# A bidirectional hybrid encoder layer: the scan's turns move from TensorE to VectorE and DMA, and the planner's step estimate is set anew

## The chip, the cores and the metric

The kernel runs on one core of one Trainium2 chip. The metric is the device time of one execution in microseconds (us), the median of several runs; less is better. TensorE (PE in the profile) does the matmuls, VectorE (DVE) and ScalarE (ACT) the elementwise work and the evacuation of PSUM, GpSimd (POOL) small work, and SyncE (SP) issues nearly all DMAs, in order, from one queue.

## What is computed

One encoder layer is applied to two request groups, 1024 and 256 tokens, with shared weights, in float32. The tokens go through one projection into three head groups: a scan in two directions (SSD, 16 heads of 64), windowed attention (8 heads of 64) and attention to a memory of 256 rows (4 heads of 128). The three results go side by side through the output projection. Cut to what bears on the change:

```python
def layer(x, mem, ...):
    proj = rms_norm(x, norm_g) @ w_in
    xbc, z_ssd, dt_raw, q, k, v, z_att, mq, z_mem = split_cols(proj, IN_SIZES)
    xbc = jax.nn.silu(centred_dwconv(xbc, conv_w, conv_b))
    xs, Bm, Cm = split_cols(xbc, ...)
    y_f = ssd_scan(xs, dt[:, :, 0], A[0], Bm, Cm)
    y_b = ssd_scan(xs[:, ::-1], dt[:, ::-1, 1], A[1], Bm[:, ::-1], Cm[:, ::-1])[:, ::-1]
    y = (y_f + y_b + d_skip[:, None] * xs).reshape(b, T, SSD_WIDTH)
    yg = (y * jax.nn.silu(z_ssd)).reshape(b, T, SSD_GROUPS, SSD_WIDTH // SSD_GROUPS)
    o_ssd = rms_norm(yg, ...)
    ...
    return x + jnp.concatenate([o_ssd, o_att, o_mem], axis=-1) @ w_out
```

## The kernel before

The 1280 tokens are ten tiles of 128 (t = 0 to 7 of the long group, 8 and 9 of the short one), in two groups of five. Every large product is done in three passes: both operands are split into a high and a low part (`wsplit`, line 338, for weights: ACT makes `wh`, DVE makes `wl`), and high x high, high x low and low x high are summed. So a weight tile `wraw` (SP's DMA, four buffers) turns into `wh` and `wl` (three buffers each) and then serves 15 matmuls, three for each of five token tiles. That is `block_tok` (line 368): 16 steps k over the 2048 input features, 512 output columns. Other products use seven multiplications for eight (`block_pair`, line 1327). The last of the projection's blocks and the output's blocks run in this order: kv, mq, z0, z1 for the first group; z0, z1, mq for the second; then four output blocks, the last two of them clear of other work; then `block_pair` for the second group of the output.

Beside the dense matmuls stand four *lanes*, queues of Python generators: `ATT` (attention, memory attention), `SSD` (`ssd_one`, `ssd_two`), `PREP` (preparations of q, k and memory) and `DEC` (`decay`). Every generator cuts its work into steps and yields `wants(tiles, banks, after)` ahead of a step: the tiles it will read, how many of the three shared PSUM banks (`mix`) it takes, and what must have been said to be done. After each piece of a dense block, `run` calls `pump` (line 301), which takes steps from the lanes in the order ATT, PREP, SSD, DEC, as far as `may` allows. All of this happens when the program is written: what decides is not the chip but `Clocks` (line 43), an estimate with one clock for each engine. `cost` (line 61) gives an instruction's time, `ran` (line 75) books it, `ready` (line 111) says whether the step's inputs are there by the clock of PE. The chip then runs the fixed order; a step put too early makes TensorE wait, one put too late makes its lane longer.

Some dates force a lane, whatever `ready` says. `refill_o` (line 1581), which loads the second operand of the output blocks during the second mq block, needs `ssd_two(5)` by k = 11; and at k = 9 of the third output block all lanes are emptied, since their memory is given back.

The scan. The convolution leaves its results in DRAM with features on rows, `xbc_d[12, 128, 1280]`. `ssd_one(t)` (line 948) loads two tiles `xc` of 128 features x 4 x 128 tokens each, one for each half of the heads, turns each by four 128x128 transposes on TensorE into a PSUM bank `pxs` (lines 974 to 977), and DVE copies it to `xs`, with tokens on rows. `ssd_two(t)` (line 1156) ends with the normed output `y`, tokens on rows. `turn_ssd` (line 1145) turns it back with four transposes into the bank `pr`, ACT copies it to `so`, and one DMA stores it to `oT_d[2 + g]`, features on rows, of shape [128, 4, 640] for each group of five tiles. `refill_o` and `seven_load` read these as rows of 640 values.

Of the kernel before, what the change touches and what calls it, by code (L numbers as in the profile page):

```python
# [19 lines left out]
P = 128  # L20
# [10 lines left out]

RATES = {'kv': (4, 4), 'mq0': (8, 8), 'z0': (8, 8), 'z1': (8, 8), 'mq1': (8, 8), 'o': (8, 8)}
DEBT = 6.0
AHEAD, QUEUE = 300.0, 4000.0
NEG = -1e30

UNITS = (0, 4, 1, 5, 2, 6, 7, 3, 8, 9)
# [5 lines left out]
class Clocks:  # L43
# [17 lines left out]
    def cost(self, e, ins, ops, power):  # L61
        n = max([self.size(x) for x in ops] or [1])
        if e == "PE":
            m = self.size(ops[0])
            one_pass = ops[-1].dtype == F32R or ops[1].dtype == F32R
            return m / 2.4 + 14 if one_pass else max(m / 0.6, 213) + 6
        if e == "DVE":
            return 150 + 1.05 * n
        if e == "ACT":
            return (190 + 0.8 * n if n > 16 else 190) + (190 if len(ins.outs) > 1 else 0)  # L70
        if e == "POOL":
            return 60 + 4.2 * n if n > 16 else 250 + 180 * n if power else 300
        return 50

    def ran(self, e, ins, power=False):
        outs, srcs = [[x.bass_ap for x in xs if hasattr(x, "bass_ap")] for xs in (ins.outs, ins.ins)]
        cost = self.cost(e, ins, outs + srcs, power)
        if e != "SP":
            self.now[e] = max(self.now[e], self.now["PE"])
        if not self.lane:  # L80
            self.now[e] += cost
            return
        at = self.now[e] if e != "SP" else self.now["PE"]
        for x in srcs:
            at = max(at, self.full.get(self.name(x), 0.0))
        for x in outs:
            at = max(at, self.free.get(self.name(x), 0.0))
        if e == "SP":
            end = at + 2600 + self.size(outs[0]) * 1.5
        else:  # L90
            end = self.now[e] = at + cost + 20
        for x in srcs:
            k = self.name(x)
            self.free[k] = max(self.free.get(k, 0.0), end)
        for x in outs:
            k = self.name(x)
            if e != "SP":
                self.free[k] = max(self.free.get(k, 0.0), end)
            self.full[k] = end + 90
# [10 lines left out]

    def ready(self, want):
        tiles, n = want[:2]
        at = [self.full.get(self.name(x), 0.0) - (0 if n else AHEAD) for x in tiles]
        at += [self.opens("mix", 3, i + 1) - 400 * i for i in range(n)]
        at += [self.now[e] - QUEUE for e in ("ACT", "DVE")]
        return max(at) <= self.now["PE"]

# [28 lines left out]
def wants(*tiles, banks=0, after=()):  # L146
    return tiles, banks, after
# [3 lines left out]
def hymba_encoder_kernel(  # L151
# [67 lines left out]
    def dram(shape, name):  # L219
        return dr.tile(shape, F32, tag=name, name=name)  # L220
# [4 lines left out]
    q_d = [dram([P, 512], f"q_{t}") for t in range(NT)]  # L225
    mq_d = [dram([P, 512], f"mq_{t}") for t in range(NT)]
    kv_d = [dram([P, 288], f"kv_{t}") for t in range(NT)]
    oT_d = [[dram([P, 4, 640], f"oT{c}_{g}") for g in range(2)] for c in range(4)]
    yp_d = [dram([P, 1024], f"yp_{t}") for t in range(NT)]
    sb_d = [dram([P, 1024], f"sb_{t}") for t in range(NT)]  # L230
    row_d = [[dram([P, 640], f"row{n}{k}") for n in "HL"] for k in range(KT)]
# [65 lines left out]
    def may(i):  # L297
        w = wanted[i]
        return owed[i] >= 1 and lanes[i] and (w is None or (said.issuperset(w[2]) and clk.ready(w)))

    def pump(rates):

        for i in range(4):
            owed[i] = min(owed[i] + rates[i % 2], DEBT) if lanes[i] else 0.0
        while True:
            i = next((j for j in (ATT, PREP, SSD, DEC) if may(j)), None)
            if i is None:
                return
            owed[i] -= 1
            step(i)  # L310
# [627 lines left out]
    def wb(name, dtype=F32, shape=(P, 512)):  # L938
        return mp.tile(list(shape), dtype, tag="wb", name=name, bufs=WBB)
# [4 lines left out]
    def prior(t, *part):  # L944
        i = SCAN.index(t)
        return (("decay", SCAN[i - 1]) + part,) if i else ()

    def ssd_one(t):
# [4 lines left out]
        S.dma_start(bc, xbc_d[8:12, :, tok].rearrange("f p c -> p f c"))  # L953
        xc = []
        for g in range(2):
            x = wb("xc", shape=(P, 4, P))
            S.dma_start(x, xbc_d[4 * g:4 * g + 4, :, tok].rearrange("f p c -> p f c"))
            xc.append(x)
        yield wants(bc, banks=1, after=prior(t, "weighed"))
        ps = psum("pcb")  # L960
# [10 lines left out]
        said.add(("ssd_one", t, "cb"))  # L971
        xsT = []
        for g in range(2):
            yield wants(xc[g], banks=1, after=prior(t) + (("dt_prep", t // 5 * 5),))
            ps = psum("pxs")
            for j in range(4):
                turned(ps[:, j * P:(j + 1) * P], xc[g][:, j, :])
            xt = mp.tile([P, 512], F32, tag="xs", name="xs", bufs=2)
            V.tensor_copy(xt, ps)
            xsT.append(xt)  # L980
        xs_of[t] = xsT
        yield wants(cb)
# [162 lines left out]
    def turn_ssd(g):  # L1145

        if g in last_y:
            t, y = last_y.pop(g)
            ps = psum("pr")
            for j in range(4):  # L1150
                T.transpose(ps[:, j * P:(j + 1) * P], y[:, j * P:(j + 1) * P], ident)
            o = mp.tile([P, 512], F32, tag="rb", name="so", bufs=RBB)
            A.activation(o, ps, AF.Copy)
            S.dma_start(oT_d[2 + g][t // 5][:, :, t % 5 * P:(t % 5 + 1) * P], hv(o, 4))

    def ssd_two(t):
        first = t in (NS - 1, NT - 1)
        last = t in (0, NS)
        tok = slice(t * P, (t + 1) * P)
        yield wants(after=(("decay", t // NS * NS),))  # L1160
        ss = sm.tile([P, 2], F32, tag="s2", name="yss", bufs=4)
        if not last:
            cc = mp.tile([P, 2, P], F32, tag="btok", name="cc", bufs=1)
            S.dma_start(cc, xbc_d[10:12, :, tok].rearrange("f p c -> p f c"))
        ld = []
        for g in range(2):
            c = slice(g * 512, (g + 1) * 512)

            y = mp.tile([P, 512], F32, tag="ya" if t % 2 else "rf", name="yd", bufs=2)
            S.dma_start(y, yp_d[t][:, c])  # L1170
            z = mp.tile([P, 512], F32, tag="xs", name="zd", bufs=2)
            S.dma_start(z, z_d[g][t])
            st = None
            if not first:
                st = state[:, c] if last else wb("st2")
                S.dma_start(st, sb_d[t][:, c])
            ld.append((y, z, st))
        yield wants(*([last_y["y"][2]] if "y" in last_y else []))
        norm_ssd()
        for g in range(2):  # L1180
            c = slice(g * 512, (g + 1) * 512)
            y, z, st = ld[g]
            yield wants(y, z, *(() if last else (cc, state)), banks=0 if last else 1)
            if not last:
                pf = psum("pyb")
                T.matmul(pf, cc[:, g, :], state[:, c], start=True, stop=True)
                y2 = wb("y3")
                V.tensor_mul(hv(y2), hv(pf), hb(eacs_all[:, t, 8 * g:8 * g + 8], 8, 64))
                V.tensor_add(y, y, y2)
            V.tensor_mul(y, y, z)  # L1190
            if not first and not last:
                V.tensor_mul(hv(state[:, c]), hv(state[:, c]), hb(cd_all[:, t, 8 * g:8 * g + 8], 8, 64))
                V.tensor_add(state[:, c], state[:, c], st)
            yield wants(y)
            A.activation(z, y, AF.Square, scale=0.5, accum_out=ss[:, g:g + 1])
            if g in last_y:
                yield wants(last_y[g][1], banks=1)
                turn_ssd(g)
        yield wants(ss)
        rs = sm.tile([P, 2], F32, tag="s2", name="yrs", bufs=4)  # L1200
        rsqrt(rs, ss, 1.0 / 512, 2)
        G.tensor_scalar(out=rs, in0=rs, scalar1=0.5, scalar2=None, op0=ALU.mult)
        last_y["y"] = t, [x[0] for x in ld], rs
        if first:
            yield wants(rs)
            norm_ssd()
            for g in range(2):
                yield wants(last_y[g][1], banks=1)
                turn_ssd(g)

    seven = {1: (0, 0, 0), 2: (0, 1, 5), 6: (1, 1, 2), 5: (1, 0, 1), 3: (1, 2, 6), 7: (0, 3, 3), 4: (0, 2, 4)}
# [2 lines left out]
    def seven_load(k):  # L1214

        q, j = divmod(k, 4)
        raw[k] = [rp.tile([P, 640], F32, tag="ch", name=n, bufs=CH) for n in ("ra", "rb_")]
        S.dma_start(raw[k][0], oT_d[q][1][:, j, :])
        S.dma_start(raw[k][1], oT_d[2 + q][1][:, j, :])

    def seven_sums(k):
        a, b = raw[k]
# [332 lines left out]
    def part(fn, *a, **kw):  # L1555
        return lambda: fn(*a, **kw)
# [24 lines left out]
    def refill_o(grp):  # L1581
        def f(q):
            need((attn, mem_attn, ssd_two, ssd_two)[q], [4 if q < 2 else 5])
            return [part(fill_direct, q, j, oT_d[q][grp][:, j, :],
                         gain=None if q < 2 else vec[:, R_SG + 4 * (q - 2) + j:R_SG + 4 * (q - 2) + j + 1])
                    for j in range(4)]
        return f
# [285 lines left out]
```

## Time and profile before

| | us |
|---|---|
| median of 3 runs | 1777.49 (1776.81 to 1780.14) |
| the profiled execution's own time | 1773.83 |
| its span, first to last instruction | 1772.1 |
| GpSimd busy | 683.8 |
| DMA, mean of the span | 177 GB/s |

The span is what lies between the first and the last instruction; 1.7 us more lie around it. A busy TensorE is not a TensorE at its peak: its matmuls are pipelined, their durations overlap, and only the distance from one start to the next tells what one costs. DVE and ACT overlap in the same way, though less. In a group's row, "x80" is the number of instructions, and three times stand for shortest, median and longest. The kernel records every instruction through one helper, line 128, so groups are told apart by their tiles. Three lines of the page that the prediction does not show:

```profile
DVE  5596788989968888797777877678776533766665
ACT  6554555445545444346787666658886532433332
DMA  8794454446544333376467766767785734644442
```

Each digit is a tenth of the busy share in one of 40 slices of 44 us; the lanes run from slice 18 to slice 33.

### The profile page before, as it was taken

What the parts mean: (1) busy time and instruction counts of PE and PEld (TensorE: products, weight loads), DVE (VectorE), ACT (ScalarE), POOL (GpSimd) and SP (SyncE); (2) the same over time, 40 slices, a digit from 0 to 9 for tenths busy, and PEclk for the clock granted to TensorE, in tenths of its full rate; (3) what the DMA queues carried; (4) which work ended last, traced back from release to release, by engine and by line L of the source; (5) the groups of instructions that cost most, each with busy time, mean ns of one, the idle gap of its engine ahead of it and who ended that gap; (6) DMA issues with size and microseconds to landing.
All of it is one profiled execution on the core that took longest, in us unless ns stands there. A gap on an engine that the chain in (4) does not pass through costs nothing.

```text
span 1772.1 us, 30974 instructions
## 1 busy us (share of the span) xinstructions
PE 1755.3 (99%) x10306; PEld 1572.0 (89%) x10306; DVE 1310.9 (74%) x2417; ACT 971.8 (55%) x2181; POOL 683.8 (39%) x1092
## 2 busy tenths in 40 slices
PE   9999999999999999999999999999999999999999
PEld 7889999999899999988788877887788888889999
DVE  5596788989968888797777877678776533766665
ACT  6554555445545444346787666658886532433332
POOL 0026798860478989220110000111200100068775
PEclk9999999999999999999999999999999999999999
DMA  8794454446544333376467766767785734644442
GB/s 293 238 319 175 136 149 148 128 143 194 156 119 145 119 104 106 90 216 208 143 188 249 259 213 192 226 190 230 243 249 161 222 110 147 207 142 147 145 144 77
DMA packets 210993, 313.23 MB, mean 177 GB/s; under 512 B 21584, under 2 KB 84368, under 8 KB 210832
## 3 DMA queue, kind: packets, MB, share of 16 engines
q1 hardware_dynamic: 210688, 311.19, 56.7%
q8 instruction: 81, 1.33, 0.3%
q14 instruction: 80, 0.66, 0.1%
q10 hardware_dynamic: 144, 0.06, 0.0%
HBM read 242.42 MB, written 68.75 MB: 176 GB/s over the span
## 4 chain that ended last, share of the span: by engine, by line
PE 88%; DMA 4%; DVE 3%; ACT 2%; issue 1%; POOL 1%; SPq 0%; ACTq 0%; DVEq 0%; POOLq 0%
PE acc L128 66%; PE accm L128 11%; PE py L128 2%; PE po L128 1%; PE psc L128 1%; PE pst L128 1%; PE pmo L128 1%; PE pms L128 1%; PE ppt L128 1%; DMA wraw<-in_w_in_laid_dram 1%; PE pyf L128 1%; DMA xst<-in_x_prompt_dram 1%; DVE wl L128 1%; PE pyb L128 0%; ACT lg L128 0%
## 5 line engine op out<-in xcount | busy, mean ns | idle before, releaser
L128 PE MATMUL acc<-wh,xH 128*128 128x512 f32 (+1 forms) x1248 | 490.0, 393 | 0.1
L128 DVE TENSOR_TENSOR wl<-wraw,wh 128x512 fp32r<-128x512 f32 (+1 forms) x480 | 355.5, 744 | 172.9 <-ACT wh L128 170.1
L128 PE MATMUL acc<-wl,xH 128*128 128x512 f32 (+1 forms) x1248 | 473.7, 380 | 0.7 <-DVE wl L128 0.5
L128 PE MATMUL acc<-wh,xL 128*128 128x512 f32 (+1 forms) x1248 | 472.1, 378 | 0.0
L128 ACT ACTIVATE wh<-wraw 128x512 fp32r<-128x512 f32 (+1 forms) x480 | 291.5, 613 | 211.6 <-PE acc L128 136.5
L128 POOL TENSOR_TENSOR ws<-wraw 128x128 f32<-128x128 f32 x224 | 156.9, 700 | 365.8 <-DMA wraw<-in_w_in_pairs_dram 163.1
L128 PEld LDWEIGHTS acc<-wl,xH 128*128 128x128 f32 x1248 | 234.7, 188 | 45.1 <-issue 6.5
L128 PEld LDWEIGHTS acc<-wh,xH 128*128 128x128 f32 x1248 | 234.6, 188 | 44.9 <-issue 7.0
L128 PEld LDWEIGHTS acc<-wh,xL 128*128 128x128 f32 x1248 | 234.2, 188 | 44.6 <-issue 1.0
L128 ACT ACTIVATE sh<-ws 128x384 fp32r<-128x384 f32 x224 | 115.5, 522 | 253.3 <-POOL ws L128 126.6
L128 DVE TENSOR_TENSOR sl<-ws,sh 128x384 fp32r<-128x384 f32 x224 | 158.7, 712 | 115.4 <-ACT sh L128 113.9
L128 POOL TENSOR_TENSOR ws<-wraw,ws 128x128 f32<-128x128 f32 x224 | 153.1, 683 | 17.2
L128 POOL TENSOR_TENSOR ws<-ws,wraw 128x128 f32<-128x128 f32 x224 | 154.3, 689 | 0.0
L128 POOL TENSOR_TENSOR wraw<-wraw 128x128 f32<-128x128 f32 x224 | 139.8, 624 | 17.1
L128 PE MATMUL acc<-xH,wl 128*128 128x320 f32 x320 | 100.0, 312 | 1.0 <-DVE wl L128 1.0
L128 PE MATMUL acc<-tH,sl 128*128 128x320 f32 x320 | 98.9, 309 | 0.0
L128 PE MATMUL acc<-xL,wh 128*128 128x320 f32 x320 | 98.9, 309 | 0.0
L128 PE MATMUL accm<-tH,wl 128*128 128x320 f32 x320 | 98.8, 309 | 0.0
L128 PE MATMUL acc<-tH,sh 128*128 128x320 f32 x320 | 98.7, 309 | 0.0
L128 PE MATMUL acc<-xH,wh 128*128 128x320 f32 x320 | 98.7, 309 | 0.0
L128 PE MATMUL accm<-tL,wh 128*128 128x320 f32 x320 | 98.5, 308 | 0.0
L128 PE MATMUL accm<-tH,wh 128*128 128x320 f32 x320 | 98.5, 308 | 0.0
(458 smaller groups left out, 3829.1 us busy)
## 6 DMA issues: line engine op xcount, KB each, us to landing
wraw<-in_w_in_pairs_dram SPq DMA_DIRECT2D x160, 256.0 KB, 2.7
wraw<-in_w_in_laid_dram SPq DMA_DIRECT2D x128, 256.0 KB, 3.6
wraw<-in_w_out_laid_dram SPq DMA_DIRECT2D x64, 256.0 KB, 3.1
wraw<-in_w_out_pairs_dram SPq DMA_DIRECT2D x64, 256.0 KB, 2.9
rf<-ac SPq DMA_DIRECT2D x40, 256.0 KB, 3.8
rb<-ac SPq DMA_DIRECT2D x40, 256.0 KB, 4.2
wraw<-in_w_mem_laid_dram SPq DMA_DIRECT2D x32, 256.0 KB, 4.7
ra<-in_x_turned_dram SPq DMA_DIRECT2D x16, 320.0 KB, 3.8
```

Source lines behind the costliest of these rows:

```text
L128: r = f(*a, **kw)
```

## The change

The diff has three parts. The scan's input tile is loaded by four DMAs, one for each 32 tokens, into the 32 rows that those tokens will have, in runs of 32 values (32x32 blocks, features on rows within a block); one DVE transpose of all 32x32 blocks then gives `xs`. The normed output is turned by one DVE transpose, and four DMAs put the blocks in their place in DRAM; the layout of `oT_d[2]` and `oT_d[3]` becomes [4, 128, 640]. Both steps take no PSUM bank any more.

The estimate gets other costs: for one-pass matmuls at least 85 ns, for others a share by the rows written; for DVE 67 + 1.04 n, for ACT 50 or 92 + 0.835 n and 92 for each further operand or output. An instruction's end no longer holds its engine for 20 ns, but its result counts as late by 110 ns (ACT) or 90 ns (DVE). A step that takes a bank is ready 700 ns after its inputs and 300 ns after the bank; one that takes none, at the time of its inputs (before: 300 ns ahead of it).

The order of the lanes becomes SSD, DEC, ATT, PREP between the end of `mem_attn(4)` and that of `ssd_two(5)`.

```diff
-AHEAD, QUEUE = 300.0, 4000.0
+MARGIN, QUEUE = {"PE": 700.0, "bank": 300.0, "other": 0.0}, 4000.0
+LATE = {"ACT": 110.0, "DVE": 90.0}
...
-            return m / 2.4 + 14 if one_pass else max(m / 0.6, 213) + 6
+            return max(m / 2.4 + 14, 85) if one_pass else max(m / 0.6, 213) * list(ops[0].ap)[0][1] / 128 + 6
         if e == "DVE":
-            return 150 + 1.05 * n
+            return 67 + 1.04 * n
         if e == "ACT":
-            return (190 + 0.8 * n if n > 16 else 190) + (190 if len(ins.outs) > 1 else 0)
+            aps = sum(hasattr(x, "bass_ap") for x in ins.ins)
+            return (50 if ops[-aps].space == "PSUM" else 92) + 0.835 * n + 92 * (aps - 1) + (92 if len(ins.outs) > 1 else 0)
...
-            end = self.now[e] = at + cost + 20
+            self.now[e] = at + cost
+            end = at + cost + LATE.get(e, 20)
...
-        at = [self.full.get(self.name(x), 0.0) - (0 if n else AHEAD) for x in tiles]
-        at += [self.opens("mix", 3, i + 1) - 400 * i for i in range(n)]
+        at = [self.full.get(self.name(x), 0.0) + MARGIN["PE" if n else "other"] for x in tiles]
+        at += [self.opens("mix", 3, i + 1) - 400 * i + MARGIN["bank"] for i in range(n)]
...
-    oT_d = [[dram([P, 4, 640], f"oT{c}_{g}") for g in range(2)] for c in range(4)]
+    oT_d = [[dram([P, 4, 640] if c < 2 else [4, P, 640], f"oT{c}_{g}") for g in range(2)] for c in range(4)]
...
-            i = next((j for j in (ATT, PREP, SSD, DEC) if may(j)), None)
+            late = ("mem_attn", 4) in said and ("ssd_two", 5) not in said
+            i = next((j for j in ((SSD, DEC, ATT, PREP) if late else (ATT, PREP, SSD, DEC)) if may(j)), None)
...
-            x = wb("xc", shape=(P, 4, P))
-            S.dma_start(x, xbc_d[4 * g:4 * g + 4, :, tok].rearrange("f p c -> p f c"))
+            x = wb("xc")
+            for a in range(4):
+                c = slice(t * P + 32 * a, t * P + 32 * a + 32)
+                S.dma_start(x[32 * a:32 * a + 32].rearrange("p (b j) -> p b j", j=32),
+                            xbc_d[4 * g:4 * g + 4, :, c].rearrange("f (q i) c -> i (f q) c", i=32))
...
-            yield wants(xc[g], banks=1, after=prior(t) + (("dt_prep", t // 5 * 5),))
-            ps = psum("pxs")
-            for j in range(4):
-                turned(ps[:, j * P:(j + 1) * P], xc[g][:, j, :])
+            yield wants(xc[g], after=prior(t) + (("dt_prep", t // 5 * 5),))
             xt = mp.tile([P, 512], F32, tag="xs", name="xs", bufs=2)
-            V.tensor_copy(xt, ps)
+            V.transpose(xt, xc[g])
...
-            ps = psum("pr")
-            for j in range(4):
-                T.transpose(ps[:, j * P:(j + 1) * P], y[:, j * P:(j + 1) * P], ident)
             o = mp.tile([P, 512], F32, tag="rb", name="so", bufs=RBB)
-            A.activation(o, ps, AF.Copy)
-            S.dma_start(oT_d[2 + g][t // 5][:, :, t % 5 * P:(t % 5 + 1) * P], hv(o, 4))
+            V.transpose(o, y)
+            for a in range(4):
+                c = slice(t % 5 * P + 32 * a, t % 5 * P + 32 * a + 32)
+                S.dma_start(oT_d[2 + g][t // 5][:, :, c].rearrange("f (q i) c -> i (f q) c", i=32),
+                            o[32 * a:32 * a + 32].rearrange("p (b j) -> p b j", j=32))
...
-                yield wants(last_y[g][1], banks=1)
+                yield wants(last_y[g][1])
...
-        S.dma_start(raw[k][1], oT_d[2 + q][1][:, j, :])
+        S.dma_start(raw[k][1], oT_d[2 + q][1][j])
...
-            return [part(fill_direct, q, j, oT_d[q][grp][:, j, :],
+            return [part(fill_direct, q, j, oT_d[q][grp][:, j, :] if q < 2 else oT_d[q][grp][j],
```

2 lines of the change are left out of this document (1 added, 1 removed).

## The prediction, made before the changed kernel had been run

> **What bounds the kernel now.** I read the page first: the shares of busy time and the chain that ended last.
>
> ```profile
> span 1772.1 us, 30974 instructions
> PE   1755.3 (99%) x10306; PEld 1572.0 (89%) x10306; DVE 1310.9 (74%) x2417; ACT 971.8 (55%) x2181; POOL 683.8 (39%) x1092
> q1 hardware_dynamic: 210688, 311.19, 56.7%
> PE 88%; DMA 4%; DVE 3%; ACT 2%; issue 1%; POOL 1%; SPq 0%; ACTq 0%; DVEq 0%; POOLq 0%
> ```
>
> TensorE leaves only 17 us of the span uncovered, and 88% of the chain is its own work. Work that leaves TensorE shortens the kernel; work added to another engine costs only where TensorE comes to wait for it. The page is an average, so I cut out the stretch in which the lanes (attention, scan, preparations) run between the dense matmuls, with the answer by windows; its columns are length, then busy time of PE, PEld, DVE, ACT, POOL, then clock, DMA share and GB/s.
>
> ```profile
> 766.00:1410.00 644.00, 634.90 (x3473) 516.54 (x3474) 486.95 (x1103) 447.81 (x1203) 76.85 (x148) 1.00 0.68 211
> 1410.00:1446.00 36.00, 36.00 (x199) 30.87 (x198) 13.64 (x29) 17.37 (x41) 0.00 (x0) 1.00 0.47 142
> ```
>
> The granted clock is 1.00, so nothing is to be won there. DVE is at 487/644 = 76% and DMA at 68%: both have room. Next, the waits of TensorE between 766 and 1450 us (total, times, longest), those of 0.5 us and more:
>
> ```profile
> PE py L128 <- ACT mpT L128: 2.3, 1, 2.3
> PE ppt L128 <- DVE nm L128: 1.4, 1, 1.4
> PE po L128 <- ACT pT L128: 0.9, 1, 0.9
> PE pms L128 <- DVE mql L128: 0.9, 1, 0.9
> PE pxs L128 <- DMA xc<-xbc_d: 0.8, 1, 0.8
> PE pms L128 <- DVE moT L128: 0.6, 1, 0.6
> PE pacs L128 <- issue: 0.5, 1, 0.5
> PE psc L128 <- ACT st L128: 0.5, 1, 0.5
> ```
>
> Together 7.9 us, nearly all at steps of the lanes, whose inputs came later than the step estimate had it. That is all a better estimate can earn there; moving the transposes must earn the rest.
>
> **The transposes that leave TensorE.** How many there are comes from the tiles' own rows, what one costs from the timeline of PE around two lone ones.
>
> ```profile
> L128 PE MATMUL pxs<-identr,xc x80: 221/248/305, 782.7 to 1331.8; 128*128 128x128 f32 x80
> L128 PE MATMUL pr<-identr,yd x80: 270/272/329, 1162.0 to 1410.0; 128*128 128x128 f32 x80
> L128 ACT ACTIVATE so<-pr x20: 576/594/602, 1162.7 to 1410.4; 128x512 f32<-128x512 f32 x20
> 1056.91 0.50 PE L128 MATMUL pxs<-identr,xc 128*128 128x128 f32 x4
> 1057.25 0.47 PE L128 MATMUL acc<-wl,xH 128*128 128x512 f32 x1
> 1057.55 0.39 PE L128 MATMUL acc<-wh,xL 128*128 128x512 f32 x1
> 1057.78 0.39 PE L128 MATMUL acc<-wh,xH 128*128 128x512 f32 x1
> 1162.03 0.60 PE L128 MATMUL pr<-identr,yd 128*128 128x128 f32 x4
> 1162.39 0.47 PE L128 MATMUL acc<-wh,xH 128*128 128x512 f32 x1
> 1162.70 0.39 PE L128 MATMUL acc<-wl,xH 128*128 128x512 f32 x1
> ```
>
> The durations overlap, so 80 x 0.272 us would count too much; starts are what a pipelined engine is to be charged by. A dense matmul takes 0.23 us from start to start (1057.55 to 1057.78). Four pr transposes push the next dense matmul from 1162.03 to 1162.39, and that one then takes 0.31 instead of 0.23 us: 0.36 + 0.08 = 0.44 us for a bank. For pxs: 0.34 + 0.07 = 0.41 us. With 80/4 = 20 banks each that is 8.8 + 8.2 = **17.0 us** off TensorE. Where a bank stands beside another lane step the 0.08 us on return stay; were that so for all, 20 x 0.36 + 20 x 0.34 = 14 us would be left, which is the low end of this term. Also 40 claims on the three shared PSUM banks go: counted at nothing, a gain at most.
>
> **What DVE and ACT take over.** The copy of pxs to xs becomes a block transpose of the same 128x512 values out of SBUF; the copy of pr, on ACT, becomes another on DVE.
>
> ```profile
> L128 DVE COPY xs<-pxs x20: 675/680/692, 785.0 to 1332.1; 128x512 f32<-128x512 f32 x20
> L128 DVE RECIPROCAL mden<-mden x20: 147/162/167, 1083.0 to 1438.2; 128x2 f32<-128x2 f32 x20
> 1160.65 0.68 DVE L128 TENSOR_TENSOR state<-state,cd_all 128x512 f32<-128x512 f32 x1
> 1161.25 0.69 DVE L128 TENSOR_TENSOR yd<-yd,y 128x512 f32<-128x512 f32 x1
> ```
>
> The trace has no block transpose. Its nearest row is the copy that it replaces, 0.68 us, and I take that: DVE gains 20 x 0.68 = 13.6 us, ACT loses 20 x 0.594 = 11.9 us. The far bound: sixteen column blocks, each as dear as a smallest DVE instruction (0.162 us), 2.6 us for one, 40 x 2.6 = 104 us less the 13.6 us of copies, so 90 us more against 644 - 487 = 157 us idle there. Below nothing: SBUF may be read faster than PSUM; a gain of a few us off the bound. Cover: TensorE's dense matmuls, whose split weights stand in three buffers. Without that cover 13.6 us would come back. The output transpose waits for a scaling on DVE itself and so adds no new wait.
>
> **The DMA pieces.** Each of 40 moves of 256 KB becomes four of 64 KB in runs of 128 bytes (32 values) instead of 512.
>
> ```profile
> xc<-xbc_d SPq DMA_DIRECT2D x20, 256.0 KB, 4.9
> oT<-so SPq DMA_DIRECT2D x20, 256.0 KB, 3.4
> kr<-kv SPq DMA_DIRECT2D x10, 64.0 KB, 2.6
> dtm<-kv SPq DMA_DIRECT2D x10, 16.0 KB, 1.8
> 1051.05 1.14 SPq L128 DMA_DIRECT2D xc<-xbc_d  x2
> SPq L128 <- DVE wl L128: 581.1, 324, 6.8
> ```
>
> 120 issues more at 1.14/2 = 0.57 us are 68 us of SP, which stands 581 us waiting for weight buffers to come free: hidden. Behind a piece on SP stand weight loads and the other lanes' loads; eight pieces in a row hold them for 8 x 0.57 - 1.14 = 3.4 us. The packets rise by 40 x (2048 - 512) = 61,440. By the page a packet takes 0.567 x 16 x 1772 / 210,688 = 0.076 us of an engine on average, at a mean of 1.5 KB, so at most 61,440 x 0.076 / 16 = 292 us of each engine, 45% of the 644 us and more than the 32% that are free; at the other end, by bytes alone, nothing. Loads of 128-byte runs are in the trace (dtm, 16 KB in 1.8 us) and look ordinary, so I lie near the low end: hidden. Stores in such runs are not in it.
>
> The transpose of xc now waits on DVE for pieces where before TensorE waited. Queued behind it stand the weight splits and all lane work of DVE, and TensorE waits for those. By the row above two loads went out from 1051.05 on, and the transposes of the second ran at 1056.91, 5.9 us later. The last of eight pieces goes out 7 x 0.57 = 4.0 us after the first and lands 2.6 us later, at 6.6 us: DVE stands up to 1 us in such tiles, one or two lane steps in each of the ten tiles may slip behind it. I charge 2 us in all.
>
> The trace has no store of short runs, so here the Trainium skill speaks against the change: "DMA: Bandwidth & Descriptors", section Specifications, asks for at least 512 B for line rate and says that below it the engine does a read-modify-write. The loads of dtm do not show it; no row shows it for stores. It is the rule beside rival E below.
>
> **The step estimate.** It sets only where the steps stand in the program. Back to back, 512 values take DVE 0.60 us (1160.65 to 1161.25). The old formula has 150 + 1.05 x 512 + 20 = 708 ns, the new one 67 + 1.04 x 512 = 599 ns, then 90 ns until the result is seen, and a matmul step waits 700 ns longer. A step behind one DVE instruction is put some 0.7 us later; behind a queue of seven (7 x 0.11) as early as before. With DVE at 76% such queues are usual, so I expect the lanes to run about as fast as now and half of the 7.9 us of waits to go: **4 us**, bounds 0 and 7.9. At the end DVE is at 13.64/36 = 38%, queues are short, and the lanes lose a little. Whether this matters is a question of dates:
>
> ```profile
> L128 SPq DMA_DIRECT2D z<-zs x20: 319/320/553, 912.8 to 1204.3; - x20
> L128 SPq DMA_DIRECT2D mq<-qs x10: 319/319/692, 822.4 to 1301.7; - x10
> 1240.67 0.60 PE L128 MATMUL pr<-identr,yd 128*128 128x128 f32 x4
> 1443.70 1.95 PE L128 MATMUL pmo<-mpT,mv 128*128 128x128 f32 x16
> 1445.65 126.25 PE acc L128 x561
> ```
>
> The second mq block runs from 1204 to 1302, 6.1 us per k, and forces ssd_two(5) at its k = 11, at 1204 + 12 x 6.1 = 1277; it is done soon after 1241 (the tenth bank of pr). All lanes are drained by force at k = 9 of the third output block. The last 561 matmuls take 0.225 us each; 480 are the two last blocks, so the third one starts 81 x 0.225 = 18 us after 1445.65 and drains 150 x 0.225 = 34 us after that, at 1498. The last lane step is at 1444. So some 35 and 52 us of slack, less the 17 us by which the blocks come sooner. The order rule between the two dates changes who goes first, not what is done: nothing.
>
> **Sum.** 1773.8 (the profiled run: span 1772.1 and 1.7 around it) - 17.0 - 4 + 2 = 1754.8. The median of the runs shown, 1777.5, lies 3.7 above the profiled run, so I forecast a median of **1758.5**.
>
> **Rivals.**
> - B, *the estimate is right at last*: all 7.9 us go and nothing is charged for pieces: 1777.5 - 17 - 8 = 1752.5. For: the waits are estimate errors. Against: DMA landings, which it still guesses.
> - C, *the lanes come late and are forced*: 0.7 us at every matmul step eats the slack, and the drain runs what is left with no dense matmul between. Two memory-attention tiles with some 6 us of waiting in each give back 12: 1770. For: the almost empty queues at the end. Against: 52 us of slack.
> - D, *the estimate does not do what it says*: costs near the true ones lose the cushion of 0.11 us in each instruction, and lane waits grow from 8 to 25 us, which eats the transposes: 1777. Against: 0.7 us of margin is six such cushions.
> - E, slower: *short runs land late and DVE, in order, stands at the xc transpose*. Were the pieces to land one after another at 2.6 us each, the eighth would come 8 x 2.6 = 21 us after the first issue, 15 us after the 5.9 us of today. Weight splits held for two k's (12 us) cover most of one such stall for the dense matmuls, not for lane steps; 4 us uncovered in each of ten tiles make 40 us: 1758.5 + 38 = 1797. It decides from a landing of 2.6 us per piece in series; at half of that it vanishes. Against: 16 engines, DMA at 68%, dtm's quick loads.
>
> **Chances.** Forecast 0.60 (its own range 1752 to 1765), B 0.10, C 0.14, D 0.06, E 0.10. What this kernel's measurements can tell from no change is about 0.2%, 3.6 us. Faster: 0.60 + 0.10 + 0.10 of C = 0.80; within: 0.04 of C and 0.06 of D = 0.10; slower: E, 0.10. The range leaves out E, half of D and of the outer edge of B: 1747 to 1775.
>
> **What would show it.** In the changed profile: no pxs and no pr; 160 matmuls fewer; a DVE transpose x40 near 0.68 us; TensorE's waits on lane steps at about 4 us; the last lane step before 1480; DVE waits on xc under 10 us in all. I am wrong if a long wait of TensorE stands in the second mq block or the third output block (C), if DVE's waits on xc grow to tens of us (E), if the transpose takes 2 us or more, or if new waits on lane inputs outgrow the old ones (D).

## The result: slower by 2.6%, and the profile after

The changed kernel takes 1823.63 us (1820.47 to 1829.56), the kernel before 1777.7 beside it: a ratio of 1.026 [1.023, 1.029]. The forecast was 1758.5. The profiled execution took 1820.47 us. From its page: span, engines, packets and SP's queue of DMAs.

```profile
span 1818.4 us, 30700 instructions
PE 1760.7 (97%) x10146; PEld 1567.8 (86%) x10146; DVE 1324.3 (73%) x2437; ACT 962.6 (53%) x2161; POOL 693.1 (38%) x1092
DMA packets 274350, 313.20 MB, mean 172 GB/s; under 512 B 105424, under 2 KB 147728, under 8 KB 274192
q1 hardware_dynamic: 274048, 311.20, 56.4%
```

160 matmuls have gone, as the change says, and yet TensorE is busy 5.4 us longer than before (1755.3), and the span holds 57.7 us in which it is not (16.8 before). The DMA engines' share did not move (56.7 to 56.4%). The profile by windows, with the same stretch as in the prediction first (columns as there):

```profile
766.00:1410.00 644.00, 598.28 (x3042) 479.52 (x3042) 467.79 (x1040) 401.43 (x1075) 74.55 (x127) 0.96 0.67 197
1200.00:1400.00 200.00, 172.94 (x834) 134.06 (x833) 139.42 (x302) 120.65 (x313) 28.05 (x49) 0.93 0.68 198
```

In the 200 us from 1200 on, TensorE stands 27 us, and the granted clock, 1.00 in the same window before, is 0.93 on average. What it waits for between 766 and 1560 us (total, times, longest), the first row:

```profile
PE acc L131 <- ACT wh L131: 37.2, 10, 10.2
```

It is new. The dense matmuls wait for `wh`, ACT's half of a split weight. ACT is busy for 53% of the span only; its own wait in the window 1325 to 1345 us names the weight's DMA:

```profile
ACT wh L131 <- DMA wraw<-in_w_out_laid_dram: 11.7, 1, 11.7
```

That is the longest case. Its timeline on SP, on DVE and on PE (start, length, engine, operation, count; in brackets the idle time before it):

```profile
1300.56 0.32 SPq L131 DMA_DIRECT2D zd<-z  x1
1305.10 0.32 SPq L131 DMA_DIRECT2D mq<-qs  x1
...
1318.08 0.50 SPq L131 DMA_DIRECT2D wraw<-in_w_out_laid_dram  x1
1318.63 0.44 SPq L131 DMA_DIRECT2D q<-q  x1
1319.11 1.49 SPq L131 DMA_DIRECT2D xc<-xbc_d  x3
1324.57 4.12 SPq L131 DMA_DIRECT2D oT<-so  x8
1328.74 2.65 SPq L131 DMA_DIRECT2D xc<-xbc_d  x5
...
1333.38 0.43 SPq L131 DMA_DIRECT2D wraw<-in_w_out_laid_dram  x1
```

```profile
1321.83 0.69 DVE L131 TENSOR_TENSOR wl<-wraw,wh 128x512 fp32r<-128x512 f32 x1 [4.83 <-ACT wh L131]
...
1323.84 0.70 DVE L131 STREAM_TRANSPOSE so<-yd 128x512 f32<-128x512 f32 x1
...
1324.52 0.69 DVE L131 STREAM_TRANSPOSE so<-yd 128x512 f32<-128x512 f32 x1
```

```profile
1331.02 0.30 PE L131 MATMUL pcb<-identr,bc 128*128 128x128 f32 x1
1341.48 0.79 PE L131 MATMUL acc<-wh,xH 128*128 128x512 f32 x1 [10.15 <-ACT wh L131]
```

The weight load of 1318.08 had itself gone out 29.4 us after the one before it. In that stretch too lie 16 pieces of the scan, but they took only 8.7 us to issue; SP stood 8.9 us before stores of `mq`, which belong to other work, 4.2 of them between the first two rows. Between the load of 1318.08 and the next, at 1333.38, stand 16 pieces of the scan and five other loads. SP is one queue in order: at 1320.6 it came to the stores of `so` and stood for 4 us, since DVE began the first of these tiles only at 1323.84. And DVE, in order too, had itself stood 4.83 us before that, at the split of a late weight. So, read from the order in time, the loss feeds itself: a late weight holds DVE, DVE's transpose then holds SP, and behind it on SP stands the next weight. That one left at 1333.38, ACT could start on it at 1340.79, and TensorE went on at 1341.48. These 7.4 us are twice the 3.6 that such a load of `w_out` takes to land at the median: three more weight loads and three of `chd` left within 7 us behind it, and in the window from 1335.7 on the DMA share is 0.90 (last section). Why it landed so late was not tested.

What the prediction had named as signs:

```profile
L131 DVE STREAM_TRANSPOSE xs<-xc x20: 671/704/707, 787.7 to 1381.2; 128x512 f32<-128x512 f32 x20
L131 DVE STREAM_TRANSPOSE so<-yd x20: 667/703/707, 1174.3 to 1449.8; 128x512 f32<-128x512 f32 x20
L131 PE MATMUL pmo<-mpT,mv x160: 271/275/343, 1131.7 to 1541.0; 128*128 128x128 f32 x160
xc<-xbc_d SPq DMA_DIRECT2D x80, 64.0 KB, 2.6
oT<-so SPq DMA_DIRECT2D x80, 64.0 KB, 2.3
wraw<-in_w_in_laid_dram SPq DMA_DIRECT2D x128, 256.0 KB, 4.0
```

The transposes cost what was booked (0.70 us). The pieces land after 2.6 and 2.3 us, the weights of the projection after 4.0 (3.6 before). The lanes' last matmul is at 1541 instead of 1444 us.

### The profile page after: what moved, and what is told of

It is laid out like the page before. It is cut to its first block, busy times and chain, and to the rows that moved or that the text cites. A ratio compares the mean times of both kernels' runs of the same rounds, so it can differ in the third digit from the quotient of the medians.

```text
span 1818.4 us, 30700 instructions
## 1 busy us (share of the span) xinstructions
PE 1760.7 (97%) x10146; PEld 1567.8 (86%) x10146; DVE 1324.3 (73%) x2437; ACT 962.6 (53%) x2161; POOL 693.1 (38%) x1092
## 3 DMA queue, kind: packets, MB, share of 16 engines
q1 hardware_dynamic: 274048, 311.20, 56.4%
## 5 line engine op out<-in xcount | busy, mean ns | idle before, releaser
L131 PE MATMUL acc<-wh,xH 128*128 128x512 f32 (+1 forms) x1248 | 495.2, 399 | 37.7 <-ACT wh L131 37.2
L131 PE MATMUL acc<-wl,xH 128*128 128x512 f32 (+1 forms) x1248 | 478.6, 383 | 2.5 <-DVE wl L131 2.5
L131 PE MATMUL acc<-wh,xL 128*128 128x512 f32 (+1 forms) x1248 | 478.2, 383 | 0.0
L131 PEld LDWEIGHTS acc<-wl,xH 128*128 128x128 f32 x1248 | 238.5, 191 | 50.5 <-DVE wl L131 6.6
L131 POOL TENSOR_TENSOR ws<-wraw,ws 128x128 f32<-128x128 f32 x224 | 153.1, 683 | 17.2
L131 POOL TENSOR_TENSOR es<-sinkb,nm 128x2 f32<-128x2 f32 x40 | 13.4, 334 | 245.3 <-DVE nm L131 182.0
```

Source lines behind the costliest of these rows:

```text
L131: r = f(*a, **kw)
```

## The experiments

Eighteen kernels ran. "Stretch" in the table is the time between the issues of two successive weight loads on SP, read from SP's timeline between 740 and 1480 us: the longest one, and how many exceed 28 us. "wh" is TensorE's whole wait for `wh`. Ratios are to the kernel before on the same chip; its medians there lie between 1775.8 and 1777.7, so two rows from different chips are to be compared by their ratios, and differences of some 2 us are not told.

| run | us | ratio [95%] | longest stretch, us | over 28 us | wh, us |
|---|---|---|---|---|---|
| before | 1777.7 | | 14.7 | 0 | 0 |
| changed kernel | 1823.63 | 1.026 [1.023, 1.029] | 30.9 | 5 | 37.2 |
| est_only | 1784.62 | 1.0044 [1.0029, 1.0059] | 14.7 | 0 | 0 |
| turns_only | 1815.9 | 1.0216 [1.02, 1.0231] | 47.8 | 3 | 23.0 |
| one_move | 1770.32 | 0.9963 [0.995, 0.9976] | 11.2 | 0 | 0.3 |
| pieces_act | 1806.31 | 1.0163 [1.0146, 1.018] | 19.2 | 0 | 3.7 |
| pieces_pool | 1984.91 | 1.1167 [1.1146, 1.1188] | 23.6 | 0 | 6.3 |
| load_pieces | 1793.22 | 1.009 [1.0073, 1.0106] | 31.8 | 3 | 16.0 |
| store_pieces | 1791.29 | 1.0082 [1.0067, 1.0097] | 29.9 | 2 | 14.1 |
| long_runs | 1776.41 | 1.0002 [0.9992, 1.0012] | 29.2 | 1 | 9.6 |
| short_runs | 1772.08 | 0.9976 [0.9964, 0.9987] | 17.2 | 0 | 0 |
| weights_first | 1816.67 | 1.0221 [1.0202, 1.024] | 18.2 | 0 | 0.3 |
| weights_first_old | 1820.64 | 1.0238 [1.0221, 1.0255] | 20.8 | 0 | 0 |
| weights_first_before | 1783.53 | 1.0038 [1.0023, 1.0052] | 12.7 | 0 | 0 |
| short_in_long_order | 1775.89 | 1.0001 [0.9991, 1.001] | 29.7 | 1 | 9.9 |
| long_in_short_order | 1820.9 | 1.0251 [1.0236, 1.0267] | 32.0 | 4 | 37.3 |
| pieces_one_order | 1781.92 | 1.0027 [1.0017, 1.0037] | 13.2 | 0 | 0 |
| after_mended | 1809.0 | 1.0172 [1.0145, 1.0198] | 21.9 | 0 | 22.4 |
| long_order_mended | 1771.44 | 0.9966 [0.9956, 0.9975] | 16.1 | 0 | 2.8 |
| turns_old_mended | 1786.67 | 1.0056 [1.0039, 1.0073] | 20.4 | 0 | 11.5 |

Two theories run through them. One blames SP's queue: first the number of DMAs on it (Q in the texts below), later (O) the order in which the queues were written out. The other, R, blames runs of 128 bytes. A word on the order: the lanes' planner says in which order instructions are emitted; a scheduler of the framework then places them on each engine's queue when the program is built, and the chip runs that.

### The two halves of the change

`est_only` is the kernel before with the new estimate and lane order, `turns_only` the changed kernel with the old ones.

> The new step estimate, margins and lane order alone; the turns stay on TensorE as before. Theory Q (the 160 small DMAs on SP's in-order queue hold weight loads behind them until TensorE runs dry): no small DMAs here, so 1768 to 1780 us and no wait of TensorE for weights over 3 us. Rival S (the new order of the lanes' steps, not the DMAs, costs the time): 1810 us or more, with the long waits for wh as in the changed kernel.

> The VectorE turns with their small DMAs alone, under the old step estimate. Q: 1795 to 1825 us, TensorE waits for wh 20 us or more in all. S: 1757 to 1765 us, the transposes gone and the old order kept.

The estimate alone costs 1784.62 - 1777.0 = 7.6 us, the turns alone 38.9; the sum, 46.5, is the loss of the whole change (45.9). From the page of the first, its first waits between 766 and 1500 us, and the first two of `turns_only`:

```profile
PE 1759.3 (99%) x10306; PEld 1572.5 (88%) x10306; DVE 1311.0 (74%) x2417; ACT 971.8 (54%) x2181; POOL 683.5 (38%) x1092
PE pxs L131 <- DMA xc<-xbc_d: 2.4, 2, 1.6
PE pxs L131 <- DVE nm L131: 1.8, 1, 1.8
```

```profile
PE acc L128 <- ACT wh L128: 23.0, 7, 8.8
PE pyb L128 <- DMA cc<-xbc_d: 7.4, 1, 7.4
```

The new estimate makes no weight wait; it spreads more small waits over the lane steps. `est_only` lies 4.6 us above the range of Q, but 25 below that of S: the new order of the steps alone does not make the loss. The weight waits come with the turns.

### Which part of the turns

`one_move` keeps both transposes on DVE but loads and stores each tile with one DMA in runs of 512 bytes, as before the change; `load_pieces` and `store_pieces` leave one side in pieces. With one move, a tile's blocks land in other places.

```diff
-            for a in range(4):
-                c = slice(t * P + 32 * a, t * P + 32 * a + 32)
-                S.dma_start(x[32 * a:32 * a + 32].rearrange("p (b j) -> p b j", j=32),
-                            xbc_d[4 * g:4 * g + 4, :, c].rearrange("f (q i) c -> i (f q) c", i=32))
+            S.dma_start(hv(x, 4), xbc_d[4 * g:4 * g + 4, :, tok].rearrange("f p c -> p f c"))
```

> The changed kernel with its VectorE transposes and its estimate, but each tile moved by one DMA in runs of 512 bytes, as before the change; blocks land in the wrong places, so the scan's numbers are not the layer's. The estimate has no clock for SP, so the steps stand in the same order. Q: 1752 to 1768 us, waits for wh under 8 us. S, and also rival V (the transposes on VectorE hold the weight splits): 1810 to 1825 us as in the changed kernel. Rival R (runs of 128 bytes are slow in the DMA engines): as Q.

> The changed kernel with small DMAs for the scan's input alone; the output is stored by one DMA a tile in runs of 512 bytes, in the wrong places, so the scan's numbers are not the layer's. Q: half of the 120 extra DMAs, so about half of the 53 us between one move and the changed kernel: 1790 to 1802 us. If only the stores (which wait for VectorE on SP) hold the queue: 1772 us.

> The changed kernel with small DMAs for the normed output alone; the input comes by one DMA a tile in runs of 512 bytes with its blocks in the wrong places, so the scan's numbers are not the layer's. Q: 1790 to 1802 us. If the loads alone hold the queue: 1772 us.

With one move per tile the kernel is faster than before: TensorE is busy 1741.9 us against 1759.3 in `est_only`, 17.4 us less, and 14.3 of them arrive in the time. That is 2.3 us above the range of Q, and V is out: the same transposes run on VectorE here. Loads in pieces cost 22.9 us on top, stores 21.0, both together 53.3: no single side is to blame, and the two make it worse together.

### Another queue for the pieces

`S.dma_start` of all 160 pieces becomes `A.dma_start` (ACT's queue) or `G.dma_start` (GpSimd's).

> The changed kernel with all 160 small DMAs issued from ScalarE's queue instead of SP's; same runs of 128 bytes, same engines that move them. Q: SP's queue is free, waits for wh fall under 10 us; ScalarE pays 160 issues of about 0.5 us, 80 us, in a stretch where it is about 70% busy: 1760 to 1785 us. R: the runs are as slow as before and the weights as late: 1810 us or more.

> The changed kernel with the 160 small DMAs in runs of 128 bytes issued from GpSimd's queue, which is almost idle in this stretch. Q: SP is free and no engine with lane work stands behind the DMAs: 1768 to 1785 us, waits for wh under 8 us. R: 1810 us or more. Rival L (a DMA landing late holds the VectorE transpose, and with it the weight splits, wherever it was issued): 1785 to 1805 us, with VectorE waits on xc of 20 us or more.

On ACT's queue the weight waits nearly vanish, but ACT is an engine with work: it now stands where a DMA instruction waits, and TensorE waits for the lane steps behind it (PE rows). DVE waits for `xc` too. From GpSimd it is far worse; its own rows show what precedes a piece there. First the run on ACT's queue, then the one on GpSimd's:

```profile
PE ppt L131 <- ACT lg L131: 9.1, 4, 3.5
ACT cb L131 <- DMA xc<-xbc_d: 18.3, 2, 9.3
DVE xs L131 <- DMA xc<-xbc_d: 21.4, 5, 6.5
```

```profile
POOL xc L131 <- issue: 190.4, 64, 6.4
POOL oT L131 <- issue: 175.7, 66, 5.1
L131 POOL DMA_DIRECT2D xc<-xbc_d x80: 651/656/886, 750.8 to 1530.4; - x80
```

190.4/64 = 3.0 us before a piece in which the profile shows no wait, and 0.66 us for the instruction: a piece occupies GpSimd for some 3.6 us, and the small scan work that lies there comes late. Moving the pieces off SP frees the weights and holds up something else. Q had 1785 us at most for both, so its ranges failed; L has its sign in the second run, where DVE waits 60.7 us for `xc`, but not its time.

### Number of DMAs, or length of runs

`long_runs` keeps 160 pieces of 32 rows, but in runs of 512 bytes; `short_runs` has one DMA per tile, in 2048 runs of 128 bytes.

```diff
+                S.dma_start(hv(x, 4)[32 * a:32 * a + 32], xbc_d[4 * g:4 * g + 4, 32 * a:32 * a + 32, tok].rearrange("f p c -> p f c"))
...
+            S.dma_start(x.rearrange("p (b j) -> p b j", j=32),
+                        xbc_d[4 * g, :, c].unsqueeze(1).broadcast_to([P, 16, 32]))
```

> The changed kernel with its 160 small DMAs of 64 KB on SP, but cut so that each moves 32 rows in runs of 512 bytes instead of 128; blocks land in the wrong places, so the scan's numbers are not the layer's. Q (the number of DMAs on SP's in-order queue): 1810 to 1830 us, as the changed kernel. R (the short runs in the DMA engines): 1768 to 1780 us, as with one move for a tile (1770).

> Each load and each store of a scan tile is ONE DMA again, as in the run with one move (1770.3 us), but cut into 2048 runs of 128 bytes as in the changed kernel (1823.6 us); what is read and where it lands is other data than the reference's. Theory O (the weight loads stand too far behind many pieces on SP's queue; the runs themselves cost little): 1768 to 1780 us, no wait for wh above 3 us. Theory R (runs of 128 bytes are slow wherever they stand): 1800 us or more, with several waits for wh of 3 us or more. Between 1780 and 1800 both count, in the share that the sum of the waits for wh has.

Neither makes the loss. The row of `short_runs` proves that the short packets are there (103,504 under 512 B, as many as in the changed kernel within 2%):

```profile
DMA packets 272431, 313.20 MB, mean 177 GB/s; under 512 B 103504, under 2 KB 145808, under 8 KB 272272
```

```profile
PE acc L131 <- ACT wh L131: 9.6, 2, 9.0
```

The second fence is `long_runs`: one long weight wait is left of ten. So many pieces cost 6 us, short runs 2 us, each against `one_move`, but together 53. That fits neither theory as it stood. The written programs gave the hint: the changed kernel and `long_runs` emit the same 1332 DMAs for SP in the same order, yet the scheduler put 446 of them at other places.

### Weights first, by the scheduler's priority

Each weight load of `block_tok` is emitted with a precedence of 400 instructions, in the changed kernel, in `turns_only` and, as a control, in the kernel before.

```diff
-            load(feats[k], raw[:, :n])
+            with tc.high_priority(offset=400):
+                load(feats[k], raw[:, :n])
```

> The changed kernel with its weight loads of the token blocks given precedence over the pieces in the order of SP's queue (at most 18 DMAs stand between two weight loads, 29 before, 3 such gaps of 12 or more instead of 13). The pieces are all there, in their runs of 128 bytes. Theory O: the waits of TensorE for wh fall under 10 us, the clock comes back to 0.99 or more, 1765 to 1785 us; what may come instead is waits for xc on VectorE. Theory R: the queue moves as slowly as before, 1805 us or more.

> The same precedence with the old step estimate and VectorE's turns in pieces (1815.9 us without the precedence). Theory O: 1755 to 1775 us, below the kernel before (1777), since the 17 us that leave TensorE then count. Theory R: 1800 us or more.

> A control: the same precedence in the kernel before, where TensorE hardly waits for weights. Both theories: 1774 to 1784 us, no change that can be told; a gain of more than 5 us here would mean that the precedence is worth something by itself and is to be taken off from the two runs beside it.

The times are those of R, while the weight waits go as O had it; the control lies within its range but loses 7.6 us by itself. The weight waits are gone from the changed kernel, and the time stays. Its waits, largest first:

```profile
PE py L131 <- DVE rb L131: 8.2, 2, 5.9
PE pyb L131 <- DVE nm L131: 4.6, 2, 3.4
PE pcb L131 <- DMA bc<-xbc_d: 4.0, 2, 2.8
```

Now TensorE waits for steps of the lanes. The priority moved everything at once, so these runs could not tell O from R; to settle it, the order had to be taken out of the scheduler's hands.

### The order exchanged

Edges that fix only an order, without a wait, were drawn between neighbours on every engine, along a list of instructions that another program's build had given. `short_in_long_order` is the changed kernel, whole and unaltered, in the order of `long_runs`; `long_in_short_order` is `long_runs` in the order of the changed kernel; `pieces_one_order` is the changed kernel in the order of `one_move`, four pieces in place of each move.

```diff
+        follows = _mybir.DependencyInfo(_mybir.DependencyClass.NoSync, _mybir.DependencyReason.DATA)
+        for names in ORDER.split(";"):
+            names = [f"I-{x}" for x in names.split() if f"I-{x}" in ISSUED]
+            for a, b in zip(names, names[1:]):
+                tc.add_manual_dep(ISSUED[b], a, follows, reason="order of an engine")
```

> The changed kernel, its 160 pieces in runs of 128 bytes untouched, but every engine's instructions are put into the order of the run with pieces of long runs (1776.4 us) by edges that fix an order and wait for nothing. So the runs' length alone is left of the difference to that run. Theory O (the order in which the queues were written out makes the loss): 1772 to 1785 us. Theory R (pieces of short runs move slowly by themselves): 1810 us or more. Between, each has its share.

> The other way round: the pieces of 32 rows in runs of 512 bytes (blocks in the wrong places), every engine in the order of the changed kernel (1823.6 us). Theory O: 1810 us or more, with the waits of TensorE for wh as in the changed kernel (37 us). Theory R: 1772 to 1785 us, waits for wh under 10 us.

> The changed kernel with every engine in the order of the run with one move (1770.3 us), each move's four pieces of 128-byte runs standing in a row in its place. Theory O: 1765 to 1785 us, waits for wh under 10 us, and it may beat the kernel before (1777). Theory R: 1805 us or more.

TensorE's first wait in the first of them, and in the second:

```profile
PE acc L134 <- ACT wh L134: 9.9, 2, 9.3
```

```profile
PE acc L134 <- ACT wh L134: 37.3, 10, 11.0
```

The loss goes with the order, all of it: 1775.89 and 1820.9, against 1776.41 and 1823.63 of the runs that the orders came from. Even the ten waits for `wh` of 37 us in all are there again. R is out: with the order held, the length of the runs makes no difference that can be told. `pieces_one_order` has no weight wait, but one of 7.0 us elsewhere and 8.2 us of DVE's for `xc`; that an order made for 40 moves does not quite fit 160 is a guess. The exchange fixed every engine, and the two orders differ not on SP alone: by the tiles in the two traces, also at 615 of DVE's 2437 places, 559 of ACT's 2161 and 213 of TensorE's 10,146. So it shows that the written order makes the loss, not that SP's queue makes all of it.

### Weight loads alone moved

Within a fixed order, weight loads of the scan's part are moved ahead until at most 16 DMAs stand between two: 14 loads in the changed kernel's own order, 9 in that of `long_runs`; the lists of the other engines stay as they were. In `turns_old_mended`, `turns_only` takes the order of its own counterpart with long runs, and 6 loads are moved.

> The changed kernel with every engine in its own order of before, but for 14 weight loads of the scan's part of the program: each is moved ahead on SP's queue until no more than 16 other DMAs stand between two weight loads (29 at most in the changed kernel). Nothing else is moved, unlike in the run where the scheduler was asked to put weights first. Theory O: the 37 us of waits for wh and the half clock behind them go, 1768 to 1785 us. If the weights' places are not what counts but the scan's own loads, which now stand further back: waits for the lanes' steps take their place, 1800 us or more.

> The changed kernel in the order of the run with pieces of long runs (1775.9 us in that order), with 9 weight loads moved ahead in the same manner (38 DMAs stood between two weight loads at most, 16 now). One wait for wh of 9.3 us is left in that order, and the half clock behind it. Theory O: both go, 1760 to 1770 us, faster than both kernels. If a weight load that stands earlier only holds up the moves behind it: 1775 us or more.

> The new turns in pieces with the OLD step estimate, in the order that the scheduler gives that program when its pieces have long runs, and 6 weight loads of the scan's part moved ahead until no more than 23 DMAs stand between two (49 before). If the price of the new estimate (7.6 us in the kernel without the turns) stands beside the turns too, the time is below the 1771.4 us of the same construction with the new estimate: 1760 to 1768 us. If the two are not additive, 1769 us or more; with waits for wh of 10 us or more left, the order is not good enough to tell.

From the waits and SP's timeline of `after_mended`, then from page, waits and windows of `long_order_mended`:

```profile
PE acc L134 <- ACT wh L134: 22.4, 9, 5.2
1212.41 0.90 SPq L134 DMA_DIRECT2D wraw<-in_w_in_laid_dram  x2
1215.73 1.95 SPq L134 DMA_DIRECT2D oT<-so  x4
...
1223.01 1.94 SPq L134 DMA_DIRECT2D oT<-so  x4
...
1227.44 0.90 SPq L134 DMA_DIRECT2D wraw<-in_w_in_laid_dram  x2
```

```profile
span 1770.7 us, 30739 instructions
PE 1743.1 (98%) x10146; PEld 1557.6 (88%) x10146; DVE 1320.6 (75%) x2437; ACT 963.3 (54%) x2161; POOL 678.6 (38%) x1092
PE acc L134 <- ACT wh L134: 2.8, 2, 2.2
766.00:1410.00 644.00, 627.28 (x3294) 505.14 (x3295) 496.35 (x1113) 432.25 (x1158) 74.14 (x144) 1.00 0.72 212
```

`long_order_mended` is the changed kernel's arithmetic and moves, entire, and beats both kernels: 1771.44 us, 0.9966 [0.9956, 0.9975], though 1.4 us above its range. It gives the account of the loss. Its span is 47.7 us shorter than the changed kernel's; TensorE's waits for `wh` are 34.4 us shorter (37.2 - 2.8), and the same 10146 matmuls are busy 17.6 us less, beside a granted clock of 0.999 on average instead of 0.986. That is 52.0, and other waits give 4.3 back.

`after_mended` gained 14.6 us and missed its mark of 1785 by 24: 22.4 us of weight waits stay, with no stretch over 22 us. What it shows is that the weights' places cost time by themselves: nothing else was moved, the waits for `wh` fell by 14.8 us, and the time by 14.6. In the rows above 15 us lie between two weight loads, of which SP stands 2.4 us before the first group of stores and 3.1 before the second (by the ends of the moves ahead of them). So the length of a stretch is not the whole measure. In the changed kernel, too, no wait for `wh` follows the stretches of 29.5 and 28.7 us that begin at 912 and 1110 us, and one of 5.0 us ends at 1222, though no piece stands between its weight load and the one before. Which other places in the changed kernel's order do the rest, on SP or on another engine, is open. `weights_first` warns against taking the weights for all of it: it had no weight waits and yet took 1816.67 us, though there every place had moved. `turns_old_mended` is undecided by its own terms: 11.5 us of weight waits are left, so whether the old estimate would be worth 7.6 us beside the turns is open as well.

## Why the prediction was wrong

**17.0 us off TensorE: right.** Its busy time falls by 17.4 us between `est_only` and `one_move`. Charging starts rather than durations was the right way; 160 x 0.27 would have promised 43.

**DVE's transposes at 0.68 us: right**, 0.70 us x40. DVE had the room.

**"120 issues more at 1.14/2 = 0.57 us are 68 us of SP, which stands 581 us waiting for weight buffers to come free: hidden": this step failed.** The sizes were near: a piece takes 0.49 us to issue. What failed is "hidden". The 581 us are time in which SP stands at a weight load, with the next weights already ahead of need; they are no reserve for a weight load that stands *behind* pieces, and behind the other lanes' stores that come late with them. There the sum is of another kind: the pieces' issue, plus each wait of a store for its producer, against the time that the split weights and the loads in flight cover. I worked out one such sum, "eight pieces in a row hold them for 8 x 0.57 - 1.14 = 3.4 us", and went no further. The trace has 15.3 us between two weight loads with 16 pieces and a stand of 4 us among them, and five stretches of 28.7 to 30.9 us. The step before, "the output transpose waits for a scaling on DVE itself and so adds no new wait", looked at DVE alone and not at SP, which waits for DVE there. I also took the order around the pieces as given. It is remade at every build, and this remaking decided between 1776 and 1824 us, with nine weight loads moved by hand 1771. What the runs show in place of "hidden" is a loss of 48 us (1823.63 against 1775.89) that goes with the written order; beside `long_order_mended` the trace has 34.4 us more of waits for weights and 17.6 us more of busy time. The weights' places on SP alone are shown for 14.6 us of it; for the rest the path through SP is read from the waits, not tested apart from the other engines' orders.

**+2 us charged for the pieces: right only where the order is good.** `long_order_mended` and `one_move` are the same by their ratios (0.9966 and 0.9963). In the order that the change got, it was 53.

**Packets, between nothing and 292 us of each engine: nothing was right.** The short runs cost no time that the exchange of orders can tell. The page "DMA: Bandwidth & Descriptors" of the Trainium skill, section Specifications, on which I had put rival E, holds against runs under 512 B; no run here shows a loss by it, stores included (`short_in_long_order`).

**-4 us from the estimate: wrong in sign.** Alone it costs 7.6 us [5.2 to 10.5 by the interval of the ratio]. That was rival D's side, though D had put 17 us on it, from 8 to 25. The bounds "0 and 7.9" excluded a loss without a reason. The run holds the order of the lanes too, which had been put at nothing; which of the constants does it, or whether that order does, was not tried.

**Dates: wrong.** The lanes' last step came at 1541, not before 1480. Only part of that goes with the stands: the last `pmo` is at 1481.1 in `est_only`, which has none of them, and at 1493.0 in `long_order_mended`. The new estimate and lane order alone made the lanes some 36 us longer, where "the lanes lose a little" had been expected.

**Rival E: wrong mechanism.** It gave 1797 and was the only slower one, but its sign was to be DVE standing at `xc` for tens of us; in the changed kernel no such row exists. It appears in that size only when the pieces leave SP (21.4 us in `pieces_act`, 60.7 in `pieces_pool`). The rival that was missing is the one that the trace shows: a weight load behind pieces and late stores in an in-order queue.

## What to carry to other kernels

Idle time of a queue is no cover for what is added to it; ask what the added DMAs stand in front of, and how long the work behind them can do without. When a scheduler writes the queues, compare the written order before and after a change, and before blaming the hardware run the new work in the old order: two such exchanged runs settled here that the order and not the length of the runs makes the loss, which twelve others had not. To tell one queue's order from another's, exchange one queue alone. Stores whose producers are late do more harm in an in-order queue than their issue time says; keep the critical loads ahead of them.

## What had not been expected of the hardware

The granted clock fell after a wait shorter than expected. Two windows of the changed kernel, up to the end of a wait of 1.8 us and behind it (first two rows), and one that begins 4.4 us into the wait of 10.15 us and ends 4.4 us behind it (third):

```profile
1055.00:1062.50 7.50, 5.82 (x35) 4.85 (x33) 2.58 (x4) 0.77 (x3) 0.00 (x0) 1.00 0.61 136
1062.60:1066.00 3.40, 3.39 (x7) 2.44 (x8) 3.40 (x8) 0.96 (x3) 0.00 (x0) 0.51 0.81 177
1335.70:1345.90 10.20, 4.42 (x10) 3.21 (x11) 4.44 (x9) 5.11 (x13) 2.06 (x3) 0.50 0.90 308
```

A wait of 1.8 us is followed by 3.4 us at half clock, in which a dense matmul takes 0.43 us from start to start instead of 0.23. The Trainium skill, "TensorE: Matmul & The Clock Gate", section "HAM oscillation — how this bites in real kernels", has the rule as no idle gaps over some 3.4 us; here half of that was enough, and in `est_only` too (1.8 us, `pxs`). Length alone does not decide: no fall followed the wait of 2.3 us in the kernel before (`py`, in the prediction), nor one of 2.6 us in `one_move`. Where a fall comes, its 3.4 us at half clock cost some 1.7 us beyond the wait itself, and I put the 17.6 us of busy time in this change's loss down to such stretches: the windows show the clock at 0.93 from 1200 to 1400 us, where it was 1.00 before.
